# Gate and up by seven block products, tokens stationary in the output, gate/up and down products

## The chip, the cores and the metric

One core of one Trainium2 chip runs the whole program. The metric is the device time of one execution in microseconds (us); three runs of the kernel before gave 935.81, 935.91 and 936.03 us, median 935.91 us. The engines are TensorE (PE, with its weight loads as PEld), VectorE (DVE), ScalarE (ACT), GpSimd (POOL) and SyncE (SP, which here only issues transfers). SBUF is the on-chip memory, PSUM the eight banks into which TensorE writes; one bank holds a 128x512 float32 tile.

## The reference

512 tokens of width 1024, one layer, float32. What matters here are the last steps:

```
h   = x + merged @ w_out                      # w_out 1024x1024
xn  = rmsnorm(h) * norm_ffn
hid = silu(xn @ w_gate) * (xn @ w_up)         # both 1024x2816
y   = h + hid @ w_down                        # w_down 2816x1024
out = rmsnorm(y) * norm_final
```

Ahead of them stand an input projection 1024 wide to 7184 columns, three recurrent mixers and three branch projections merged with sigmoid gates. Those are the same in both kernels.

## The kernel before, in words

Every product of large matrices is computed in three passes. A float32 operand is split into a high part (a cast to a shorter float format, by ACT, line 73) and a low part (operand minus high part, by DVE, line 74); `mm3` (lines 100 to 103) adds high*high, high*low and low*high in PSUM. A weight chunk is 128x1024 (512 KB): `wdma` (line 83) loads it into one of three buffers `wraw`, `wsplit` (line 86) splits it into one of three buffers `whi` and `wlo`. So a transfer waits until an older chunk has been split, and a split waits until TensorE is done with an older chunk.

Up to the merge the features lie on partitions and the tokens, 512 of them, are what streams. From there to the end it stays so: for each of eight feature tiles `hsrc` (line 648) takes one weight chunk, does 24 matmuls of 128x512 with the weight block as the stationary side, adds the residual (line 656), multiplies by the norm weight, splits (lines 665 to 668) and adds up squares. Then for each of 22 hidden tiles, gate and up each take one chunk and 24 matmuls (lines 678 to 685), 1056 in all; the row norm's factor is formed beside the first of them (lines 686 to 691) and applied after the product (line 693). The hidden tile is split at once (line 699). The down product takes 66 matmuls for each of eight feature tiles (line 738); the last of these tiles is done in two halves of 256 tokens (`products`, line 744), so that the final norm of the first half and its output lie beside the second. The second half is transposed on TensorE (line 775), scaled and written out.

The program is written once as a stream; a planner then orders it for each engine. It gives an engine, at each point of its own planned time, the ready instruction that stands first in the written order. An instruction whose buffer is still held, or whose input is planned to come later, is passed over, and later written work goes ahead of it. The chip then runs each engine's list strictly in that order.

Of the kernel before, what the change touches and what calls it, by code (L numbers as in the profile page):

```python
# [21 lines left out]
TK = (5, 11)  # L22
# [17 lines left out]
OUT_SHAPE = (2, L * D // 2)  # L40

# columns of the small-vector table
# [5 lines left out]
def trunk_kernel(ctx: ExitStack, tc: tile.TileContext, xT, vecs, w_main, w_v, w_r, w_gk, w_br, w_out, w_gu,  # L48
                 w_down, masks, diag, rot, out):
    nc = tc.nc  # L50
    cpool = ctx.enter_context(tc.tile_pool(name="cpool", bufs=1))
    xpool = ctx.enter_context(tc.tile_pool(name="xpool", bufs=1))
    wpool = ctx.enter_context(tc.tile_pool(name="wpool", bufs=3))
    tpool = ctx.enter_context(tc.tile_pool(name="tpool", bufs=8))
    spool = ctx.enter_context(tc.tile_pool(name="spool", bufs=39))
    mix = ExitStack()
    mpool = mix.enter_context(tc.tile_pool(name="mpool", bufs=2))
    psp = ctx.enter_context(tc.tile_pool(name="psp", bufs=4, space=bass.MemoryType.PSUM))
# [74 lines left out]
    def col(i):  # L133
        return vec[:, i:i + 1]

# [31 lines left out]
    uh, ul = [], []  # L167
    S1 = tpool.tile([P, L], F32, tag="ssum", name="ssum", bufs=1)
# [130 lines left out]
    def carried(ks, qsel, lam, pa, vs, h0, pos):  # L299
        """ks: one tile per head, or one tile holding both heads; lam: a state's decay over each tile, or None"""  # L300
# [42 lines left out]
    # a pair of heads: two full-height heads (A), or two half-height heads in one tile with the queries  # L343
    # laid out block-diagonally (C)
# [6 lines left out]
    def gated(qs, ks, fs, vs, h0, pos):  # L351
# [12 lines left out]
        tots = [tpool.tile([P, L], F32, tag="tot", name="tot", bufs=2) for _ in fs]  # L364
# [9 lines left out]
        else:  # L374
            # an even token's own score comes with level 2, an odd one's with level 4, where keys are still as they were
# [72 lines left out]
    def head_out(pss, gn, gs, o, h0):  # L448
        """normalise over each head's values (tokens on partitions), turn, scale, gate, split"""
# [196 lines left out]
    hT = []  # L646

    def hsrc(dt):
        wh, wl = wload(w_out[dt], KT, P)
        xr = temp(name="xres")  # L650
        nc.scalar.dma_start(xr, xT[:, dt, :])
        ps = psj()
        for kt in range(KT):
            mm3(ps, wh[:, kt, :], wl[:, kt, :], mh[kt], ml[kt], kt == 0, kt == KT - 1)
        h = slot(name="hT")
        nc.vector.tensor_tensor(h, ps, xr, op=ALU.add)
        hT.append(h)
        return h

    xh, xl = [], []  # L660
    S2 = tpool.tile([P, L], F32, tag="ssum", name="ssum", bufs=1)
    for dt in range(KT):
        h = hsrc(dt)
        xw = temp(name="xw")
        nc.vector.tensor_scalar(xw, h, col(V_NFFN + dt), None, op0=ALU.mult)
        hi = xpool.tile([P, L], F32R, tag=f"xh{dt}", name=f"xh{dt}")
        lo = xpool.tile([P, L], F32R, tag=f"xl{dt}", name=f"xl{dt}")
        split(xw, hi, lo)
        xh.append(hi)
        xl.append(lo)  # L670
        add_square(S2, h, dt == 0)
    rc2 = cpool.tile([P, NT], F32, tag="rc2", name="rc2")
    R2 = xpool.tile([P, L], F32, tag="R", name="R2")

# [1 line left out]
    hpool = ctx.enter_context(tc.tile_pool(name="hpool", bufs=16))  # L676
    hid = []
    for ft in range(FT):
        pss = []
        for g in range(2):  # L680
            wh, wl = wload(w_gu[g, ft], KT, P)
            ps = psj()
            for kt in range(KT):
                mm3(ps, wh[:, kt, :], wl[:, kt, :], xh[kt], xl[kt], kt == 0, kt == KT - 1)
            pss.append(ps)
            if ft == 0 and g == 0:
                ss2 = psm((P, NT))
                sumsq(ss2, S2, True, True)
                rroot(ss2, D, rc2)
            elif ft == 0:  # L690
                nc.scalar.copy(R2, bcast(rc2))
        z = temp(name="fz")
        nc.vector.tensor_tensor(z, pss[0], R2, op=ALU.mult)  # L693
        nc.scalar.activation(z, z, AF.Silu)
        hr = temp(name="hr")
        nc.vector.tensor_tensor(hr, pss[1], z, op=ALU.mult)  # L696
        a = slot(dtype=F32R, name="hh")
        b = hpool.tile([P, L], F32R, tag="h", name="hl") if ft < 16 else slot(dtype=F32R, name="hl")
        split(hr, a, b)
        hid.append((a, b))  # L700

# [1 line left out]
    HW = L // 2  # L703
    out_f = out[0].rearrange("(k p l) -> k p l", p=P, l=HW)
    out_t = out[1].rearrange("(t p d) -> t p d", p=P, d=D)
    ss3 = [psm((P, 2)) for _ in range(2)]
    r3 = [cpool.tile([P, 2], F32, tag=f"r3{i}", name=f"r3{i}") for i in range(2)]
    parts = ((0, 8), (8, 15), (15, 22))

    S3 = tpool.tile([P, L], F32, tag="ssum", name="ssum", bufs=1)  # L710

    def residual(ps, dt, cs):
        d = temp((P, cs.stop - cs.start), name="d")
        nc.vector.tensor_tensor(d, ps, R2[:, cs], op=ALU.mult)
        nc.vector.tensor_tensor(hT[dt][:, cs], d, hT[dt][:, cs], op=ALU.add)
        if dt < KT - 1:
            add_square(S3, hT[dt], dt == 0)
            return None
        sq = temp((P, HW), name="sq")
        nc.vector.tensor_tensor(sq, hT[dt][:, cs], hT[dt][:, cs], op=ALU.mult)  # L720
        return sq

    def mean(half, sq):
        sumsq(ss3[half], S3[:, half * HW:half * HW + HW], True, False)
        sumsq(ss3[half], sq, False, True)
        rroot(ss3[half], D, r3[half])

    for dt in range(KT):
        ws = []
        last = dt == KT - 1  # L730
        if not last:
            ps = psj()
        for lo, hi in parts:
            wh, wl = wload(w_down[dt, :, lo:hi, :], hi - lo, P)
            ws.append((wh, wl))
            if not last:
                for kt in range(lo, hi):
                    mm3(ps, wh[:, kt - lo, :], wl[:, kt - lo, :], hid[kt][0], hid[kt][1], kt == 0, kt == FT - 1)
        if not last:
            residual(ps, dt, slice(0, L))  # L740
            continue
        pss = [psj((P, HW)) for _ in range(2)]

        def products(half, k0, k1):
            cs = slice(half * HW, half * HW + HW)
            for (lo, hi), (wh, wl) in zip(parts, ws):
                for kt in range(max(lo, k0), min(hi, k1)):
                    mm3(pss[half], wh[:, kt - lo, :], wl[:, kt - lo, :], hid[kt][0][:, cs], hid[kt][1][:, cs],
                        kt == 0, kt == FT - 1)

        products(0, 0, FT)
        sq = residual(pss[0], dt, slice(0, HW))
        products(1, 0, TK[0])
        mean(0, sq)
        products(1, TK[0], TK[1])
        rb = bcast(r3[0])
        for d in range(KT):
            y = temp((P, HW), name="y")
            nc.vector.scalar_tensor_tensor(y, hT[d][:, :HW], col(V_NFIN + d), rb, op0=ALU.mult, op1=ALU.mult)
            (nc.scalar if d % 2 else nc.sync).dma_start(out_f[d], y)  # L760
# [17 lines left out]
        for d in range(KT - 1):  # L778
            turn(d)
# [101 lines left out]
```

## Time and profile before

| what | us |
|---|---|
| median of three runs | 935.91 |
| span of the profiled execution, first to last instruction | 933.8 |
| output projection, from 517.3 | 43.6 |
| gate and up, from 560.9 | 241.2 |
| down product, from 802.1 | 121.9 |
| end, from 924.0 | 9.8 |
| TensorE busy over the span | 921.1 |
| DVE busy over the span | 442.2 |
| ACT busy over the span | 306.7 |

For the profiled execution only the span is listed; the median of the runs lies 2.1 us above it (start and finish that the records don't hold). In the profile, the busy time of a matmul is modelled and overlaps that of the next, so the pace of TensorE is read from the starts of neighbouring matmuls. "Idle before" and "waits" name what an engine waited for last.

### The profile page before, as it was taken

The numbers are of one execution on the slowest core, as the hardware profiler recorded it, in microseconds if no ns is written. First come the engines' busy times: TensorE is split into PE (matmuls) and PEld (weight loads), VectorE is DVE, ScalarE is ACT, GpSimd is POOL, SyncE is SP. The second block draws the span as 40 slices with busy tenths as digits, with TensorE's granted clock in tenths as the row PEclk, the third lists the DMA queues.
The fourth block names the chain that finished last, engine by engine and source line by source line (L and its number), as shares of the span: only waits on it lengthen the run. The fifth ranks groups of instructions, "written<-read, shape, count | busy, mean of one in ns | idle before, by whom it ended". The sixth has DMA issues, their size and how long they took to land.

```text
span 933.8 us, 11094 instructions
## 1 busy us (share of the span) xinstructions
PE 921.1 (99%) x4520; PEld 764.7 (82%) x4520; DVE 442.2 (47%) x637; ACT 306.7 (33%) x431; POOL 76.3 (8%) x68
## 2 busy tenths in 40 slices
PE   8999999999999999999999999999999999999996
PEld 7888878888878878888888888888888888888886
DVE  7924555666453664445343564444344344233333
ACT  6444338234323223222233433332232232222220
POOL 2101102123000000111122000000000000000000
PEclk9999999999999999999999999999999999999999
DMA  8332211232221222222232452222322322323312
GB/s 289 115 113 91 91 46 46 68 91 91 91 71 65 91 68 68 91 68 68 91 113 90 132 153 93 98 91 97 107 91 91 111 92 85 105 82 105 98 46 91
DMA packets 27843, 88.26 MB, mean 95 GB/s; under 512 B 3440, under 2 KB 4880, under 8 KB 27792
## 3 DMA queue, kind: packets, MB, share of 16 engines
q1 hardware_dynamic: 25264, 83.36, 27.6%
q10 hardware_dynamic: 2016, 3.15, 1.1%
q0 software_dynamic: 512, 1.05, 0.5%
q8 instruction: 35, 0.57, 0.2%
q14 instruction: 16, 0.13, 0.0%
HBM read 84.39 MB, written 2.10 MB: 93 GB/s over the span
## 4 chain that ended last, share of the span: by engine, by line
PE 94%; DVE 2%; issue 2%; DMA 1%; ACT 1%; SPq 0%; POOLq 0%; POOL 0%; DVEq 0%; ACTq 0%
PE pj L101 26%; PE pj L102 26%; PE pj L103 26%; PE pj L234 5%; PE pm L361 1%; PE pm L358 1%; PE pm L336 1%; PE pm L234 1%; PE pm L339 1%; DMA xraw<-in_xT_dram 1%; PE pm L397 1%; ACT whi L73 1%; PE pm L469 1%; DVE pta L411 0%; DVE wlo L74 0%
## 5 line engine op out<-in xcount | busy, mean ns | idle before, releaser
L73 ACT CAST whi<-wraw 128x1024 fp32r<-128x1024 f32 (+1 forms) x153 | 158.3, 1035 | 505.2 <-PE pj L102 350.0
L101 PE MATMUL pj<-xh,whi 128*128 128x512 f32 x768 | 302.4, 394 | 0.0
L102 PE MATMUL pj<-xl,whi 128*128 128x512 f32 x768 | 299.9, 391 | 0.0
L103 PE MATMUL pj<-xh,wlo 128*128 128x512 f32 x768 | 299.5, 390 | 0.0
L74 DVE TENSOR_TENSOR wlo<-wraw,whi 128x1024 fp32r<-128x1024 f32 (+1 forms) x153 | 188.3, 1232 | 211.1 <-ACT whi L73 206.5
L103 PEld LDWEIGHTS pj<-xh,wlo 128*128 128x128 f32 x768 | 144.2, 188 | 30.0
L101 PEld LDWEIGHTS pj<-xh,whi 128*128 128x128 f32 x768 | 144.3, 188 | 29.7 <-issue 0.3
L102 PEld LDWEIGHTS pj<-xl,whi 128*128 128x128 f32 x768 | 144.3, 188 | 28.8
L101 PE MATMUL pj<-hh,whi 128*128 128x512 f32 (+1 forms) x198 | 72.5, 366 | 0.0
L103 PE MATMUL pj<-hh,wlo 128*128 128x512 f32 (+1 forms) x198 | 72.4, 365 | 0.0
L102 PE MATMUL pj<-hl,whi 128*128 128x512 f32 (+1 forms) x198 | 72.4, 365 | 0.0
L696 DVE TENSOR_TENSOR hr<-pj,fz 128x512 f32<-128x512 f32 x22 | 15.2, 692 | 72.0 <-PE pj L103 71.3
L103 PEld LDWEIGHTS pj<-hh,wlo 128*128 128x128 f32 x198 | 37.3, 189 | 6.0
L102 PEld LDWEIGHTS pj<-hl,whi 128*128 128x128 f32 x198 | 37.4, 189 | 6.0
L101 PEld LDWEIGHTS pj<-hh,whi 128*128 128x128 f32 x198 | 37.3, 189 | 6.0
L693 DVE TENSOR_TENSOR fz<-pj,R 128x512 f32<-128x512 f32 x22 | 15.2, 691 | 55.0 <-PE pj L103 55.0
L101 PE MATMUL pj<-oh,whi 128*128 128x512 f32 x96 | 38.7, 403 | 0.0
L102 PE MATMUL pj<-ol,whi 128*128 128x512 f32 x96 | 37.5, 391 | 0.0
L103 PE MATMUL pj<-oh,wlo 128*128 128x512 f32 x96 | 37.5, 391 | 0.0
L509 POOL TENSOR_TENSOR mrg<-mrg,mt 128x512 f32<-128x512 f32 x16 | 24.7, 1545 | 121.1 <-DVE mt L508 121.1
L147 POOL TENSOR_TENSOR r<-rm,mhalf 128x2 f32<-128x2 f32 x2 | 1.4, 696 | 357.5 <-DVE rm L146 357.5
L101 PE MATMUL pj<-mh,whi 128*128 128x512 f32 x64 | 24.9, 389 | 0.0
(207 smaller groups left out, 968.7 us busy)
## 6 DMA issues: line engine op xcount, KB each, us to landing
wraw<-in_w_main_dram SPq DMA_DIRECT2D x52, 512.0 KB, 3.3
wraw<-in_w_gu_dram SPq DMA_DIRECT2D x44, 512.0 KB, 3.3
wraw<-in_w_down_dram SPq DMA_DIRECT2D x16, 448.0 KB, 3.3
wraw<-in_w_br_dram SPq DMA_DIRECT2D x12, 512.0 KB, 3.3
wraw<-in_w_v_dram SPq DMA_DIRECT2D x11, 512.0 KB, 4.3
wraw<-in_w_out_dram SPq DMA_DIRECT2D x8, 512.0 KB, 3.5
wraw<-in_w_down_dram SPq DMA_DIRECT2D x8, 512.0 KB, 3.5
xraw<-in_xT_dram SPq DMA_DIRECT2D x8, 256.0 KB, 6.0
```

The lines of the kernel that those rows point to most:

```text
L73: a = nc.scalar.copy(hi, raw)
L74: b = nc.vector.tensor_tensor(lo, raw, hi.bitcast(F32), op=ALU.subtract)
L101: nc.tensor.matmul(ps, lhsT=ah, rhs=bh, start=start, stop=False)
L102: nc.tensor.matmul(ps, lhsT=ah, rhs=bl, start=False, stop=False)
L103: nc.tensor.matmul(ps, lhsT=al, rhs=bh, start=False, stop=stop)
L234: nc.tensor.matmul(pss[t], lhsT=a[kt][:, t * P:(t + 1) * P], rhs=b[:, k, :], start=kt == 0 and n == 0, stop=kt == KT - 1 and n == 2)
L336: nc.tensor.matmul(ps[:, t, :], lhsT=pa[:, h, t, :], rhs=vs[t][:, hs], start=t == 0, stop=False)
L339: nc.tensor.matmul(ps[:, t, :], lhsT=q, rhs=sts[h % n][r, t - 1, :], start=False, stop=t == NT - 1)
L358: nc.tensor.matmul(out, lhsT=ks[0][:, j], rhs=isel(qs[0]), start=True, stop=True)
L509: nc.gpsimd.tensor_tensor(mrg[dt], mrg[dt], t, op=ALU.add)
L693: nc.vector.tensor_tensor(z, pss[0], R2, op=ALU.mult)
L696: nc.vector.tensor_tensor(hr, pss[1], z, op=ALU.mult)
```

## The change

After the merge the sides of the products are swapped: a block of 128 tokens is the stationary side, and 512 (or 256) columns of the weights stream. Three stages are rewritten.

Output projection: two halves of 256 tokens, each with four PSUM banks (two token tiles by two column halves) filled over eight chunks of `w_out`. All of `w_out` is so loaded and split twice. `hnat` adds the residual, spills h to memory (8 transfers of 256 KB on the POOL queue), `hturn` transposes it back (32 transposes in all) with the norm weight applied by ACT.

Gate and up: the normalised input is cut into a 2x2 grid (token halves by halves of the 1024 inputs), the weights into a 2x2 grid (halves of the inputs by gate and up). Seven block products replace the eight, on sums of blocks. Four sums of token blocks are formed once (`combine`), and with the three plain blocks that are used they are split (`form`); four sums of weight blocks are formed on DVE for each 512 hidden columns. Hidden columns are taken in five jobs of 512 and one of 256. Each product is 24 matmuls; partial results pass between PSUM banks by ACT copies (`seed`) and DVE additions (`after`). The hidden tiles come out with tokens on partitions, and `turn_hid` transposes them (88 transposes in all).

Down product: per token half, 22 chunks of `w_down`, 12 matmuls each, all of `w_down` loaded and split twice; the hidden tiles are split here, by halves. In the second half the last four chunks are kept, so that one token tile ends before the other. Squares come from ACT with a running sum, `finish` scales and writes.

The pool of the earlier stages (`spool`, 39 tiles) is closed after the token blocks are split; the weights' second buffers `wr2`, the weight sums `wv` and the hidden tiles take its memory and wait for its tiles one by one.

```diff
+    def combine(a, b, flip=False):
+        out = []
+        for g in range(2):
+            s = slot(name="xs")
+            if flip:
+                nc.vector.scalar_tensor_tensor(s, a[g], -1.0, b[g], op0=ALU.mult, op1=ALU.subtract)
+            else:
+                nc.vector.tensor_tensor(s, a[g], b[g], op=ALU.subtract)
+            out.append(s)
+        return out
...
+    PRODUCTS = {"P1": ("11", "11"), "P2": ("12", "21"), "P5": ("R1", "V1"), "P6": ("F2", "V2"), "P7": ("S3", "V3"),
+                "P3": ("F4", "22"), "P4": ("22", "V4")}
+    SUMS = {"V1": ("11", "12"), "V2": ("V1", "22"), "V3": ("12", "22"), "V4": ("V2", "21")}
...
+        for p in ("P1", "P2", "P5", "P6", "P7", "P3", "P4") if j == 0 else ("P1", "P5", "P6", "P2", "P7", "P3", "P4"):
+            steps.append((j, p))
...
+    def prep(j, p):
...
+            if name in SUMS:
+                a, b = (live[j, s + g] for s in SUMS[name])
+                v = fw.tile([P, 1024], F32, tag="wv", name="wv", bufs=4)
+                nc.vector.tensor_tensor(v, a, b, op=ALU.add)
...
+            split(r, hi, lo)
...
+    for kt, _ in enumerate(oproj(1, second_half)):
+        if kt == 1:
+            hsquares(0, hs)
+        if 1 <= kt < 5:
+            c, g = turns[kt - 1]
+            hturn(0, hs, c, g, psj())
+            if g:
+                form("1" + "12"[c], block(0, c))
+        if kt == 5:
+            prep(0, "P1")
+    hs = hnat(1, second_half)
...
+    product(0, "P1", A, True)
+    after(0, "P1")
+    for c, g in turns:
+        hturn(1, hs, c, g, psm())
+    r1 = combine(block(1, 1), block(1, 0))
+    form("R1", r1)
+    s3 = combine(block(0, 0), block(1, 0))
+    f2 = combine(s3, block(1, 1), True)
+    form("F2", f2)
+    form("S3", s3)
+    form("F4", combine(f2, block(0, 1), True))
+    form("22", block(1, 1))
+    hsquares(1, hs)
+    late.close()
...
+    prep(*steps[1])
+    for i in range(1, len(steps)):
+        j, p = steps[i]
+        if i + 1 < len(steps):
+            prep(*steps[i + 1])
+        product(j, p, bank_of(p), p in ("P1", "P5"))
+        after(j, p)
+        if p in ("P1", "P5"):
+            turn_hid()
+            turn_hid()
```

In `product`, each product takes its weights in two halves a and b of 12 matmuls (one half for the last job). `after` does two 128x512 ACT copies behind P1, P5 and P7, two DVE additions behind P6 and P7, two Silu (ACT) behind P2 and P4, and two gated multiplications (DVE) each behind P3 and P4.

## Rows read from the trace of the kernel before

**Rows 1.** Windows: length, busy PE, PEld, DVE, ACT, POOL, clock, DMA share, GB/s.

```profile
15.00:20.00 5.00, 5.00 (x24) 4.12 (x23) 5.00 (x10) 4.75 (x11) 1.49 (x1) 1.00 1.03 399
...
517.30:560.90 43.60, 43.60 (x194) 36.03 (x193) 26.61 (x37) 16.43 (x24) 2.33 (x1) 1.00 0.52 156
560.90:802.10 241.20, 241.20 (x1074) 200.03 (x1073) 98.94 (x114) 72.44 (x92) 1.02 (x1) 1.00 0.29 96
802.10:924.00 121.90, 121.90 (x608) 103.92 (x607) 44.42 (x57) 29.38 (x37) 0.70 (x1) 1.00 0.28 82
```

**Rows 2.** The chain of waits: share by engine, then pieces (start, length).

```profile
PE 94%; DVE 2%; issue 2%; DMA 1%; ACT 1%; SPq 0%; POOLq 0%; POOL 0%; DVEq 0%; ACTq 0%
...
34.60 2.72 PE pj L234 x12
...
440.42 0.87 PE pm L469 x8
...
566.44 0.79 PE pm L140 x8
...
572.83 0.89 PE pm L155 x8
```

**Rows 3.** Timeline of TensorE: start, length, line; neighbouring 128x512 and 128x256 matmuls.

```profile
498.73 0.39 PE L103 MATMUL pj<-oh,wlo 128*128 128x512 f32 x1
498.96 0.39 PE L101 MATMUL pj<-oh,whi 128*128 128x512 f32 x1
...
912.05 0.28 PE L103 MATMUL pj<-hh,wlo 128*128 128x256 f32 x1
912.17 0.28 PE L101 MATMUL pj<-hh,whi 128*128 128x256 f32 x1
```

**Rows 4.** Groups by shape, gate and up window: busy us, mean ns, idle before.

```profile
L74 DVE TENSOR_TENSOR wlo<-wraw,whi 128x1024 fp32r<-128x1024 f32 x43 | 52.7, 1225 | 10.7 <-ACT whi L73 7.9
L73 ACT CAST whi<-wraw 128x1024 fp32r<-128x1024 f32 x43 | 45.3, 1054 | 163.5 <-PE pj L102 83.0 <-issue 80.5
L696 DVE TENSOR_TENSOR hr<-pj,fz 128x512 f32<-128x512 f32 x21 | 14.5, 692 | 68.4 <-PE pj L103 67.6 <-ACT fz L694 0.7
L74 DVE TENSOR_TENSOR hl<-hr,hh 128x512 fp32r<-128x512 f32 x21 | 14.4, 685 | 0.7 <-ACT hh L73 0.7
L691 ACT COPY R<-pm 128x512 f32<-128x512 f32 x1 | 0.6, 592 | 0.0
```

**Rows 5.** Groups by shape, whole span.

```profile
L764 ACT ACTIVATE hw<-hT,vec 128x256 f32<-128x256 f32 x7 | 3.4, 492 | 0.0
```

**Rows 6.** Timeline of DVE and ACT in the output projection.

```profile
534.96 1.22 DVE L74 TENSOR_TENSOR wlo<-wraw,whi 128x1024 fp32r<-128x1024 f32 x1
...
535.14 0.61 ACT L73 CAST xh<-xw 128x512 fp32r<-128x512 f32 x1
...
536.10 0.69 DVE L74 TENSOR_TENSOR xl<-xw,xh 128x512 fp32r<-128x512 f32 x1
```

**Rows 7.** Transfers: tile, queue, count, size, median us to landing.

```profile
wraw<-in_w_gu_dram SPq DMA_DIRECT2D x44, 512.0 KB, 3.3
...
out_dram<-y ACTq DMA_DIRECT2D x2, 256.0 KB, 3.3
```

**Rows 8.** Windows at the end, columns as in rows 1.

```profile
926.00:927.00 1.00, 0.69 (x6) 0.45 (x5) 0.16 (x1) 0.00 (x0) 0.31 (x1) 1.00 0.00 0
...
930.00:931.00 1.00, 0.00 (x0) 0.00 (x0) 0.00 (x0) 0.00 (x0) 0.00 (x0) 1.00 1.02 383
931.00:932.00 1.00, 0.00 (x0) 0.00 (x0) 0.00 (x0) 0.00 (x0) 0.00 (x0) 0.53 0.79 287
```

**Rows 9.** Timeline of the end: last matmul, mean, root, scaling, transfers.

```profile
923.82 0.28 PE L103 MATMUL pj<-hh,wlo 128*128 128x256 f32 x1
...
926.69 0.70 POOL L147 TENSOR_TENSOR r<-rm,mhalf 128x2 f32<-128x2 f32 x1 [8.28 <-DVE rm L146]
...
928.20 1.00 ACTq L789 DMA_DIRECT2D out_dram<-y  x2
```

More of the change, by code (lines that the diff above doesn't have):

```diff
@@ L363, in gated @@
         cur = [f[:, :] for f in fs]
[L364 removed]
+        tots = [mpool.tile([P, L], F32, tag="tot", name="tot", bufs=2) for _ in fs]
         if wide:
@@ L662, in trunk_kernel @@
[L662 to L673, printed above, removed]
@@ L676, in trunk_kernel @@
[L676 to L700, printed above, removed]
@@ L703, in trunk_kernel @@
[L703 to L721, printed above, removed]
@@ new lines, in hnat @@
+    def hnat(H, pss):
+        hs = []
+        for c in range(2):
+            row = []
+            for tl in range(2):
+                t = 2 * H + tl
+                xr = temp(name="xres")
+                nc.sync.dma_start(xr, x[t, :, c * HALF:(c + 1) * HALF])
+                h = slot(name="hn")
+                nc.vector.tensor_tensor(h, pss[tl][c], xr, op=ALU.add)
+                nc.gpsimd.dma_start(hspill[t, c], h)
+                row.append(h)
+            hs.append(row)
+        return hs
@@ new lines, in form @@
+    def form(name, parts):
+        hi = xform.tile([P, 4, 256], F32R, tag=f"h{name}", name="fh")
+        lo = xform.tile([P, 4, 256], F32R, tag=f"l{name}", name="fl")
+        for g in range(2):
+            split(parts[g].rearrange("p (k t) -> p k t", t=256), hi[:, 2 * g:2 * g + 2], lo[:, 2 * g:2 * g + 2])
+        forms[name] = (hi, lo)
+    def combine(a, b, flip=False):
+        out = []
+        for g in range(2):
+            s = slot(name="xs")
[5 more added lines that the diff above has]
+        return out
@@ new lines, in trunk_kernel, with product @@
+    A = B = E = None
+    def product(j, p, banks, start):
+        n = JOBS[j]
+        f, name = PRODUCTS[p]
+        fh, fl = forms[f]
+        gs = groups(j)
+        k = 4 // len(gs)
+        for gi, g in enumerate(gs):
+            wh, wl = (t.rearrange("p (k n) -> p k n", n=n) for t in live[j, "p" + name + g])
+            for tl in range(2):
+                ts = slice(tl * P, (tl + 1) * P)
+                for kk in range(k):
+                    kt = gi * k + kk
+                    for q, (x_, w_) in enumerate(((fh, wh), (fl, wh), (fh, wl))):
+                        nc.tensor.matmul(banks[tl][:, :n], lhsT=x_[:, kt, ts], rhs=w_[:, kk, :],
+                                         start=start and kt == 0 and q == 0, stop=kt == 3 and q == 2,
+                                         skip_group_check=True)
@@ new lines, in trunk_kernel, with turn_hid, silu @@
+    hidT, pending = [], []
+    def turn_hid():
+        if not pending:
+            return
+        hn, i = pending.pop(0)
+        ps = psm()
+        for t in range(NT):
+            nc.tensor.transpose(ps[:, t * P:(t + 1) * P], hn[t][:, i * P:(i + 1) * P], dg[:, 0, :])
+        r = fw.tile([P, L], F32, tag="hid", name="hid", bufs=FT)
+        nc.scalar.copy(r, ps)
+        hidT.append(r)
+    def silu(bank, n, t):
+        z = temp(name="fz")
+        nc.scalar.activation(z[:, :n], bank[:, :n], AF.Silu, scale=rc2[:, t:t + 1])
+        return z
@@ new lines, in trunk_kernel @@
+    hs = hnat(1, second_half)
+    A, B = [psj() for _ in range(2)], [psj() for _ in range(2)]
+    for tl in range(2):
+        nc.tensor.matmul(B[tl], lhsT=forms["11"][0][:, 0, :P], rhs=live[0, "p11a"][0][:, :512], start=True, stop=True)
+    product(0, "P1", A, True)
[6 more added lines that the diff above has]
+    f2 = combine(s3, block(1, 1), True)
@@ new lines, in trunk_kernel @@
+    form("F2", f2)
[4 more added lines that the diff above has]
+    late.close()
+    fw = late2.enter_context(tc.tile_pool(name="fw", bufs=1, side="right", reuse_waits="tile"))
+    m2 = cpool.tile([P, NT], F32, tag="m2", name="m2")
+    nc.vector.tensor_tensor(m2, ss2[:, :NT], ss2[:, NT:], op=ALU.add)
+    rroot(m2, D, rc2)
+    nc.gpsimd.tensor_scalar(nrc2, rc2, -1.0, 0.0, op0=ALU.mult, op1=ALU.add)
+    E = [psm() for _ in range(2)]
```

276 lines of the change are left out of this document (191 added, 85 removed).

## The prediction

> **What bounds the kernel now.** First the windows by stage: in the three stages that are rewritten TensorE is busy for the whole of 43.6, 241.2 and 121.9 us, while DVE has work for 26.6, 98.9 and 44.4 us and ACT for less [rows 1]. Then the chain of waits: 94% of it is TensorE, and no other engine holds more than 2% [rows 2]. So in these stages time is the number of matmuls by their pace. Their modelled length (0.39 us) is not the pace; the starts of neighbours are. They stand 0.23 us apart at 512 columns, and twelve with weights streaming take 2.72 us, which is 0.2267 us each; at 256 columns the step is 0.12 us [rows 2, 3]. In the twelve of 2.72 us the tokens already are the stationary side, so turning the sides round costs nothing by itself. Then the groups of DVE and ACT, because all that the change adds beside the matmuls falls on these two [rows 4, 5].
>
> **TensorE, step by step.**
> Gate and up: 1056 matmuls at 0.2267 are 239.4 us. After: five jobs of 7 x 24 at 0.2267 (190.4 us), one of 7 x 24 at 0.12 (20.2 us), 210.6 us in all: -28.8 us. The last job falls short of half by 1.1 us, because 0.12 is more than half of 0.2267.
> Transposes: 32 of h and 88 of hidden tiles. Eight took 0.87 us on the chain [rows 2], 0.11 each: +13.2 us. All stand in TensorE's order between matmuls, so none is hidden.
> Two matmuls that only open the banks B: +0.45 us.
> Gone: the row norm's sums and its spread beside the first gate product, 0.79 and 0.89 us [rows 2]: -1.7 us.
> Down product: 121.9 us now [rows 1], of which the last feature tile pays 132 steps of 0.12 and two norm steps. After, 528 at 0.2267 are 119.7 us: -2.2 us.
> The output projection keeps its 192 matmuls: 0.
> The end: from the last matmul at 923.82 to the start of the last transfers at 928.20 are 4.4 us, two per queue [rows 9]. After: addition 0.69, squares 0.6, two small DVE steps of some 0.2, root 0.70, two scalings of 0.7 and some six hand-overs of 0.1 are 4.4 us too, but the last transfer (3.3 us [rows 7]) has none ahead of it in its queue: -0.4 us (-1 to +1).
> Sum of TensorE's work: -28.8 + 13.2 + 0.45 - 1.7 - 2.2 - 0.4 = -19.45 us.
>
> **The output projection's supply.** A chunk now serves 12 matmuls, 2.72 us, where it served 24. Per chunk ACT needs 1.05 and DVE 1.23 [rows 4]; landing, cast and subtraction make 3.3 + 1.05 + 1.23 = 5.6 us for three buffers [rows 4, 7], 1.9 us a chunk. 512 KB in 2.72 us is 193 GB/s, where one window of before moved 399 GB/s [rows 1]. That holds in the down product too, where the hidden tile's split adds about half of 0.69 to DVE. Near the end of the second half the first product's two weight halves hold two of three buffers, and the last two chunks stand out: cast and subtraction behind the freed buffer, 2.3 us, then a late transfer on top, 3.2 us. The first product's 24 matmuls (5.44 us) are ready and can go in between: the trace shows the planner doing such a thing, a later chunk's subtraction at 534.96 ahead of the token tile's at 536.10, whose cast came only at 535.14 [rows 6]. I take 0 (0 to 5.4).
>
> **The crossing into gate and up, the one large stall.** When the output projection ends, DVE owes: 8 combinations and 10 low parts of 128x512, 18 x 0.69 = 12.4 us; one low part for P2 (1.23; its other half's buffer may lie free early); for P5 two additions and a low part of 128x1024, 3.7 us, an SBUF addition being priced as the subtraction of that size [rows 4]. That is 17.3 us. It can begin about 1.6 us in: the last residual additions, then the 16 transposes (1.8 us) and ACT's scalings at 0.49 each [rows 5], of which the first two must land. Add 0.7 for gaps, since the four scaled tiles come 0.9 us apart: P5 starts at about 19.6 us. TensorE has 1.76 us of transposes and P2, 5.44 us, for that time. Stall: 12.4 us. It does not matter for the sum whether P2 goes early or late. Before, there was no stall here. From below, 7 us: DVE fits low parts into the gaps and P5's needs ahead of S3, F4 and 22; what is then late next are those forms, as DVE carries job 0's own 30 us besides. From above, 17: a second-buffer load waits for a tile of the closed pool, then 3.3 us to land.
>
> [...]
>
> **Gate and up in steady state.** Per job of 512, TensorE: 168 x 0.2267 + 16 x 0.11 = 39.8 us. DVE: 14 low parts and 8 additions at 1.225, 8 steps on PSUM at 0.69: 32.5 us. ACT: 14 casts at 1.054 and 14 copies or Silus at about 0.59: 23.1 us [rows 4]. So DVE goes from 41% of the stage [rows 1] to 82% and stays below TensorE. Its worst window is the one behind P6 or P7: two PSUM steps, two additions and two low parts make 6.3 us against a product of 5.44. But the additions may be done a product earlier: four buffers, and the products between need 2.5 us. Three split buffers for two halves a product leave each half one product's length, 5.4 us, for 1.05 + 1.23 and its turn on DVE. In the window from 15 to 20 us DVE was busy all 5.00 us and TensorE too [rows 1], so a full DVE doesn't by itself stop it. Loss: at best 0; the upper bound is 12, a third of a microsecond for each of 38.5 products. I take 2. Transfers: 4 MB a job, 105 GB/s, no limit.
>
> Crossing into the down product: the banks B are free once the last Silu (0.6 us) has read them: +0.5 (0 to 2). The spill, 8 transfers, and its reading back lie beside products.
>
> **Sum.** -19.45 + 12.4 + 2 + 2 + 0.5 = -2.55 us on the profiled span of 933.8: 931.25. The runs' median lies 2.1 us above that span, and I carry that over: 933.4 us.
>
> **Rivals.**
> A, the crossing is covered. For it: DVE has room while the second half of the output projection runs, and ACT is half idle there [rows 1]. Against it: the tiles that it needs exist only after that half. With 7 for 12.4 and no clock loss: 933.4 - 5.4 - 2 = 926.0. Chance 0.20.
> B, slower: DVE becomes the bound in gate and up. It runs in strict order and waits for ACT's cast ahead of each low part (7.9 us over 43 now [rows 4]) and for TensorE ahead of each PSUM step. Its slack is 39.8 - 32.5 = 7.3 us a job, 1.04 us a product; beyond that it sets the pace. If standing takes 1.3, each of 38.5 products loses 0.3: 11.5 us in place of 2, 943 us. It decides the sign from some 0.17 us a product on (another 4.4 us over 38.5 products, beside my 2). Against it: the window with DVE full. Chance 0.27.
> C, the loads hold the crossing: the second buffers' memory comes free only with the last forms, transfers stand in order on SP, and P2, P5 and P6 each wait. The upper end of 17 and the 2.3 and 3.2 us of the output projection unfilled: 933.4 + 4.6 + 5.4 = 943.4. Chance 0.08.
> My forecast, with the crossing at 10 to 15 us and gate and up keeping pace: 0.45, its own range 929 to 938.
>
> **How the numbers follow.** A run is told from no change beyond 0.2%, 1.9 us: below 934.0 or above 937.8. The forecast puts 0.25 below, 0.13 between, 0.07 above; A all 0.20 below; B and C about 0.05 between and below together, 0.30 above. Faster 0.46, same 0.17, slower 0.37. All low ends together make 923 (7 for 12.4, no clock, no loss, 1 at the end), all high ends 960. The range, 921 to 947, allows two more below for what no row shows, and leaves out the far end of B and C above.
>
> **What would show it.** TensorE: between the output projection and gate and up an idle stretch of about 12 us with DVE busy all through, and a clock of one half behind it; before the last two chunks of the output projection no gap. Per job some 40 us with DVE at 80% and TensorE without gaps; if TensorE's starts step by more than 0.2267 ahead of each product and its releaser is DVE's low part, it is B. From the start of the down product to the last matmul some 120 us. Wrong would be a crossing under 5 us, jobs above 42 us, or transposes away from 0.11.

## The result, and the profile after

The changed kernel takes 949.38 us (median of four runs, 948.47 to 949.98) against 935.92 of the kernel before on the same chip (four runs, 935.81 to 936.03): a ratio of 1.0143 (1.0128 to 1.0157). It is slower, by 13.5 us; the forecast was 933.4, and the range ended at 947. The profiled execution has a span of 946.7 us, 12.9 more than before.

First the windows of the changed kernel, cut where its stages begin; columns as in [rows 1].

```profile
0.00:526.26 526.26, 520.86 (x2626) 423.12 (x2627) 268.29 (x423) 186.87 (x278) 72.75 (x64) 1.00 0.27 89
526.26:580.97 54.71, 54.71 (x251) 44.02 (x249) 28.65 (x30) 29.37 (x49) 6.74 (x9) 1.00 0.64 219
580.97:601.60 20.63, 9.15 (x25) 6.85 (x25) 17.06 (x26) 11.59 (x22) 2.13 (x2) 0.67 0.42 150
601.60:816.80 215.20, 214.05 (x1048) 177.93 (x1046) 167.64 (x164) 120.63 (x156) 0.00 (x0) 1.00 0.29 98
816.80:939.70 122.90, 122.90 (x530) 99.45 (x530) 77.44 (x106) 62.20 (x100) 1.86 (x3) 1.00 0.62 202
610.00:810.00 200.00, 199.88 (x965) 165.83 (x964) 154.81 (x151) 109.78 (x141) 0.00 (x0) 1.00 0.29 98
...
590.00:595.00 5.00, 0.47 (x1) 0.47 (x2) 5.00 (x10) 2.17 (x3) 0.36 (x1) 0.50 0.12 31
595.00:600.00 5.00, 5.00 (x14) 3.90 (x14) 3.88 (x4) 1.05 (x1) 1.77 (x2) 0.53 0.99 351
```

The first line is the surprise. Up to the output projection nothing was rewritten, and that part takes 526.3 us where it took 517.3 [rows 1]: +9.0. From there to the down product it is 290.5 against 284.8 (+5.7), the down product 122.9 against 121.9 (+1.0), and the end 7.0 against 9.8 (-2.8). Together +12.9. So two thirds of the loss stand where the diff has no computation, at a granted clock of 1.00 and with TensorE as busy as before (520.86 of 526.26 us, 511.72 of 517.30 before).

The chain of waits (start, length) shows what is slower there:

```profile
PE 93%; DVE 3%; ACT 1%; issue 1%; DMA 1%; SPq 0%; DVEq 0%; POOLq 0%; ACTq 0%
...
32.31 2.81 PE pm L238 x12
35.12 2.82 PE pj L238 x12
37.94 2.81 PE pm L238 x12
```

Twelve products take 2.81 us that took 2.72 [rows 2]. It is the same at every stage: over the whole trace the mean step from the start of one 512-column matmul to the next (steps over 300 ns left out) is 232.7 ns, before it was 227.2. On some 3,340 products 5.6 ns make up to 18.7 us, more than the whole loss. What the two kernels differ in there is where the operands lie. Before, in all but 18 of these products (small ones of the mixers) the program's addresses put both operands 64 bytes above a multiple of 256: normed tokens from 21056, weights from 55872, slots (the tiles of `spool`) from 115520. In the changed kernel the small constant tiles take 64 bytes more, the pools stand in another order and the slots are packed from the top of memory: weights begin at 128 above a multiple of 256, tokens at 0, slots at 224.

The crossing into gate and up, the timeline of TensorE:

```profile
579.06 1.91 PE L694 MATMUL pm<-dg,hn 128*128 128x128 f32 x16
587.69 0.80 PE L793 MATMUL pj<-whi,fh 128*128 128x512 f32 x1 [6.72 <-ACT whi L77]
...
589.13 0.63 PE L793 MATMUL pj<-whi,fl 128*128 128x512 f32 x1
594.53 0.80 PE L793 MATMUL pj<-wlo,fh 128*128 128x512 f32 x1 [4.76 <-DVE wlo L78]
595.12 0.63 PE L793 MATMUL pj<-whi,fh 128*128 128x512 f32 x1
595.54 0.63 PE L793 MATMUL pj<-whi,fl 128*128 128x512 f32 x1
...
599.76 0.39 PE L793 MATMUL pj<-wlo,fh 128*128 128x512 f32 x1
```

Two waits, 6.72 and 4.76 us, stand ahead of P2's products, and the products behind them step by 0.43 us until 599.4. The window 580.97 to 601.60 above holds only P2: 20.6 us for 5.4 us of work. The last two windows show why: DVE is busy for all 5.00 us in which TensorE has one product, and the granted clock is at 0.50 and 0.53.

Gate and up by groups, for the window 601.6 to 816.8 (busy us, mean ns, idle before):

```profile
L78 DVE TENSOR_TENSOR wlo<-wv,whi 128x1024 fp32r<-128x1024 f32 x43 | 52.5, 1223 | 22.2 <-ACT whi L77 21.1 <-PE pm L806 0.5
L77 ACT CAST whi<-wv 128x1024 fp32r<-128x1024 f32 x43 | 45.0, 1050 | 40.8 <-PE pj L793 28.4 <-PE pm L793 10.4 <-issue 1.3
L806 PE MATMUL pm<-dg,hnat 128*128 128x128 f32 x88 | 11.7, 272 | 0.0
```

The split of a weight sum costs what the split of a loaded weight cost (1223 ns on DVE and 1050 on ACT, 1225 and 1054 [rows 4]), and ACT still waits for TensorE, not the other way round.

### The profile page after: what moved, and what is told of

It reads as the page before. It is cut to its first block, busy times and chain, and to the rows that moved or that the text cites. A ratio compares the mean times of both kernels' runs of the same rounds, so it can differ in the third digit from the quotient of the medians.

```text
span 946.7 us, 11541 instructions
## 1 busy us (share of the span) xinstructions
PE 921.7 (97%) x4476; PEld 751.4 (79%) x4476; DVE 561.5 (59%) x752; ACT 411.4 (43%) x602; POOL 84.0 (9%) x79
## 4 chain that ended last, share of the span: by engine, by line
PE 93%; DVE 3%; ACT 1%; issue 1%; DMA 1%; SPq 0%; DVEq 0%; POOLq 0%; ACTq 0%
PE pj L793 16%; PE pj L105 15%; PE pj L106 15%; PE pj L107 15%; PE pm L793 6%; PE pj L238 5%; PE pm L105 3%; PE pm L107 3%; PE pm L106 3%; PE pm L365 1%; PE pm L362 1%; PE pm L238 1%; PE pm L340 1%; PE pm L343 1%; PE pm L806 1%
## 5 line engine op out<-in xcount | busy, mean ns | idle before, releaser
L105 PE MATMUL pj<-xh,whi 128*128 128x512 f32 x416 | 167.2, 402 | 0.0
L106 PE MATMUL pj<-xl,whi 128*128 128x512 f32 x416 | 164.8, 396 | 0.0
L107 PE MATMUL pj<-xh,wlo 128*128 128x512 f32 x416 | 164.7, 396 | 0.0
L793 PE MATMUL pj<-whi,fh 128*128 128x512 f32 (+1 forms) x240 | 92.4, 385 | 6.8 <-ACT whi L77 6.7
L793 PE MATMUL pj<-wlo,fh 128*128 128x512 f32 (+1 forms) x240 | 90.9, 380 | 4.8 <-DVE wlo L78 4.8
L107 PEld LDWEIGHTS pj<-xh,wlo 128*128 128x128 f32 x416 | 78.3, 188 | 18.0
L105 PEld LDWEIGHTS pj<-xh,whi 128*128 128x128 f32 x416 | 78.3, 188 | 17.6 <-issue 0.3
L106 PEld LDWEIGHTS pj<-xl,whi 128*128 128x128 f32 x416 | 78.4, 188 | 17.3
L793 PE MATMUL pj<-whi,fl 128*128 128x512 f32 (+1 forms) x240 | 91.5, 381 | 0.0
L78 DVE TENSOR_TENSOR wlo<-wv,whi 128x1024 fp32r<-128x1024 f32 x44 | 53.7, 1223 | 22.2 <-ACT whi L77 21.1
L77 ACT CAST whi<-wv 128x1024 fp32r<-128x1024 f32 x44 | 46.1, 1050 | 46.4 <-PE pj L793 28.4
```

What stands on the lines that cost most here:

```text
L77: a = nc.scalar.copy(hi, raw)
L78: b = nc.vector.tensor_tensor(lo, raw, hi.bitcast(F32), op=ALU.subtract)
L105: nc.tensor.matmul(ps, lhsT=ah, rhs=bh, start=start, stop=False)
L106: nc.tensor.matmul(ps, lhsT=ah, rhs=bl, start=False, stop=False)
L107: nc.tensor.matmul(ps, lhsT=al, rhs=bh, start=False, stop=stop)
L793: nc.tensor.matmul(banks[tl][:, :n], lhsT=x_[:, kt, ts], rhs=w_[:, kk, :], start=start and kt == 0 and q == 0, stop=kt == 3 and q == 2, sk ...
```

## The experiments

Theory T says that the pace of a 512-column product depends on whether its two operands begin at the same offset within 256 bytes. Its rivals: the offset of one operand alone counts (R1), or the slower pace has nothing to do with offsets (R2: other engines, the region of memory).

**e1, matmuls alone.** A kernel of its own: 64 groups of 24 products, every pairing of eight offsets. In short:

```
for a in RES: for b in RES:      # 0, 32, ... 224 bytes: moving, stationary
    24 x matmul(ps, lhsT=sta[:, b/4 + 128*(n%7):], rhs=mov[:, a/4 + 512*(n%3):])
```

> A kernel of matmuls alone (it computes nothing of the reference): 64 groups of 24 products of a 128x128 stationary and a 128x512 moving tile, fp32r, with all other engines idle. The moving operand begins 0, 32, ... 224 bytes behind a fixed place, the stationary one likewise, every pairing once. Theory T (the pace of a 512-column product depends on whether both operands begin at the same offset within 256 bytes; in the kernel before both do, at 64; in the changed kernel they begin 128, 96 or 32 apart): about 227 ns from start to start in the pairs with equal offsets, 232 to 234 ns in the others. Rival R1 (the offset of one operand alone counts, whatever the other's): fast rows or fast columns in the 8 by 8 table instead of a diagonal. Rival R2 (the slower pace comes from what the other engines and the DMAs do at the same time, or from the region the tiles lie in): one pace in all 64 groups.

Mean step in ns, worked out from the starts in its trace (inside each group, steps at the lower clock left out), rows the moving operand's offset, columns the stationary one's:

```
        0     32     64     96    128    160    192    224
  0  228.4  233.2  233.3  234.1  233.4  233.5  229.0  233.2
 32  233.3  227.7  233.2  233.3  234.1  233.3  233.5  229.0
 64  228.8  233.3  226.6  233.2  233.3  234.1  233.3  233.5
 96  233.3  228.9  233.3  226.7  233.2  233.4  234.1  233.3
128  233.3  233.5  229.0  233.3  226.7  233.2  233.4  234.1
160  234.0  232.4  233.2  228.9  233.2  226.6  233.2  233.3
192  233.4  234.1  233.3  233.5  229.0  233.3  226.7  233.2
224  232.8  233.3  234.1  233.3  233.5  229.0  233.3  226.7
```

The diagonal is fast (226.6 to 228.4 ns), and the table repeats along it (232.4 to 234.1 at all other differences but one), so in these 64 pairs only the difference of the offsets counts, modulo 256. R1 would have shown fast rows or columns, R2 one number; DVE, ACT and POOL had no work in this stretch:

```profile
40.00:300.00 260.00, 260.00 (x1122) 210.34 (x1121) 0.00 (x0) 0.00 (x0) 0.00 (x0) 1.00 0.00 1
```

One other difference is nearly as fast: a stationary operand that begins 192 bytes above the moving one (modulo 256), 228.8 to 229.0. That was not expected.

**e2, the changed kernel with its operands aligned.**

```
+    edge = ctx.enter_context(tc.tile_pool(name="edge", bufs=1, side="right"))
+    edge.tile([P, 56], F32, tag="pad", name="pad")
+    cpool.tile([P, 32], F32, tag="pad", name="pad")
+    tpool.tile([P, 32], F32, tag="pad", name="pad", bufs=1)
     late = ExitStack()
```

> The changed kernel with three unused tiles added (128 bytes behind the constants, 128 bytes behind the temporaries, 224 bytes at the top of memory), so that all operands of the 512-column products begin at offset 0 within 256 bytes; no instruction differs. Theory T: the step goes from 232.3 to 227 ns in all stages, 3,340 products x 5.4 ns = 18 us, so 930 to 932 us, and the first output projection at 517 us again instead of 526. Rival R2 (traffic of other engines, region of memory): 949 us, step 232, the first output projection at 526.

Measured: 932.71 us (931.91 to 933.46), 0.9968 of before (0.9955 to 0.9981), that is 16.7 us less than the changed kernel for three unused tiles, and a little above the 930 to 932 that were expected. The step is back at 227 ns in its chain (twelve products of the front, 24 of gate and up, eight transposes); below that its windows:

```profile
35.49 2.72 PE pj L242 x12
...
649.18 5.44 PE pm L797 x24
...
665.51 0.87 PE pm L810 x8
```

```profile
0.00:518.14 518.14, 511.90 (x2627) 421.95 (x2627) 269.20 (x423) 186.51 (x278) 71.65 (x64) 1.00 0.26 91
518.14:571.70 53.56, 53.56 (x251) 43.87 (x249) 28.63 (x30) 29.12 (x48) 6.72 (x9) 1.00 0.65 223
571.70:592.00 20.30, 8.79 (x26) 6.54 (x26) 17.17 (x26) 11.68 (x22) 3.21 (x2) 0.66 0.39 149
592.00:803.26 211.26, 209.98 (x1047) 177.58 (x1045) 166.47 (x164) 120.79 (x156) 0.00 (x0) 1.00 0.29 101
803.26:923.80 120.54, 120.53 (x530) 99.07 (x530) 77.51 (x106) 62.37 (x100) 1.86 (x3) 1.00 0.58 205
610.00:800.00 190.00, 190.00 (x954) 161.51 (x954) 147.06 (x146) 107.08 (x138) 0.00 (x0) 1.00 0.28 95
```

Against the changed kernel's windows the front gives back 8.1 us, the stretch up to the down product 5.4 and the down product 2.4. The crossing is as long as it was. No instruction differs, only the pace, and the 16 us between the two spans (946.7 and 930.8) are its price.

**e3, the kernel before with its weights shifted.**

```
+    gap = ctx.enter_context(tc.tile_pool(name="gap", bufs=1))
+    gap.tile([P, 32], F32, tag="pad", name="pad")
     wpool = ctx.enter_context(tc.tile_pool(name="wpool", bufs=3))
```

> The kernel before with one unused tile of 128 bytes ahead of the weight buffers: the weights and all that lies behind them begin at offset 192 within 256 bytes, the normed activations (xh, xl) stay at 64. 2,400 products then pair 192 with 64 (the first projections, gate and up), 1,134 pair 192 with 192 (output and down projections and some of the first). Theory T (equal offsets are fast, whatever they are): the 2,400 step at 232 to 233, the others stay at 227; 2,400 x 5.5 = +13 us, so 949 us; the loss stands before the output projection and in gate and up, none in the output projection (517.3:560.9 before) and the down projection. Rival R1 (offset 64 itself is fast): all 3,534 slower, +19 us, 955 us. Rival R2: 936 us, no change.

Measured: 949.93 us, 1.0155 of before (1.0138 to 1.0172). The rewriting isn't needed to get the loss. Windows by stage:

```profile
0.00:524.48 524.48, 518.57 (x2627) 422.18 (x2627) 269.28 (x423) 186.30 (x278) 71.60 (x64) 1.00 0.26 90
524.48:568.20 43.72, 43.72 (x194) 36.16 (x193) 26.61 (x37) 16.53 (x24) 2.33 (x1) 1.00 0.52 154
568.20:815.90 247.70, 247.70 (x1071) 199.62 (x1070) 98.95 (x114) 72.37 (x91) 1.02 (x1) 1.00 0.27 93
815.90:937.90 122.00, 122.00 (x607) 103.91 (x606) 44.42 (x57) 29.40 (x37) 0.69 (x1) 1.00 0.27 81
```

The two stages whose pairs stayed equal (192 with 192) keep their 43.7 and 122.0 us [rows 1]; the front (+7.2) and gate and up (+6.5), where 2,400 products became pairs of 64 with 192, pay. That is the contrast inside one kernel that T asked for, and it refutes R1, by which all four would pay.

**e4 and e11, which pair it is.** Both are matmuls alone. e4 tries offsets of 4 bytes and pairs that alternate; `group` takes the offsets of the moving and of the stationary tile. In short:

```
for b in range(0, 64, 4): group((0,), (b,))
group((0, 128), (0, 128)); group((0, 128), (128, 0)); group((0,), (0, 128))
group((0,), (0,), 256); group((0,), (128,), 256)
```

> A kernel of matmuls alone (it computes nothing of the reference), 24 products a group, fp32r. First 16 groups: moving tile at offset 0, stationary tile 0, 4, 8, ... 60 bytes behind it. Then pairs of offsets that alternate from product to product: (0 with 0, 128 with 128), where each product has equal offsets but its stationary tile differs from the moving tile of the product before; (0 with 128, 128 with 0), where it is the other way round; and moving always 0 with stationary 0, 128, 0, .... Then 256 columns at equal offsets and 128 apart. Theory T as run e1 left it: only equal offsets are fast, so 227 ns in the first group and 233 from 4 bytes on; rival: the offset counts in steps of 32 bytes, so 227 up to 28 and 233 from 32 on. For the alternating groups, theory T1 (a tile of weights is read while the product before it still streams, so a stationary tile has to match the moving tile of the product ahead of it): 233 in the first alternating group, 227 in the second. Rival T2 (a product's own two operands have to match): 227 in the first, 233 in the second. With 256 columns the time lost is the same 5.5 ns (113 to 119 ns) if it is lost at the change of weights, half of it if it is lost along the columns.

Four bytes are enough: 232.3 ns at 4, and 230 to 235 at all others up to 60, where the group with equal offsets that was measured last settles at 227. The alternating groups came out at 236.7 (own pair equal) and 230.0 (own pair unequal): the order that T1 asks for, but 3 to 4 ns above it in both. At 256 columns the one unequal pair that was tried is not slower, 120.0 equal and 118.4 unequal: both terms of the expectation are wrong. e11 lets the pair change only every twelve products:

```
run((0, 0), (0, 0)); run((0, 0), (128, 128)); run((0, 0), (0, 128)); run((0, 0), (128, 0))
```

> A kernel of matmuls alone (it computes nothing of the reference): four stretches of 384 products, 128x512 fp32r, in which twelve products with one pair of offsets (moving, stationary) follow twelve with another: (0,0) throughout; (0,0) and (128,128); (0,0) and (0,128); (0,0) and (128,0). Read is the mean step from each of the 24 places to the next. Theory T1 (what counts is the stationary tile of the next product against the moving tile that streams): in the second stretch the steps at places 11 and 23, where the pair changes, are slow (over 230 ns) and the other 22 at 227; in the third the slow ones are 11 to 22, not 12 to 23. Rival T2 (a product's own pair counts): no slow step in the second stretch, and 12 to 23 in the third. In the fourth both have 12 to 23 slow.

```
(0,0)/(128,128), median step in ns at the places 0 to 23:
231 227 226 227 227 226 227 227 226 227 227 232   231 227 226 227 227 226 227 227 226 227 227 232
```

T2 is out, since each product's own pair is equal here. The step ahead of a change is slow (232), as T1 says, but the step behind it is slow too (231). In the third stretch places 11 to 22 are slow as T1 has it (228 to 241), but 23 is too (233), and places 0 to 6 (224 to 236) stand before the pace settles at 227 from 7 on. In the fourth, places 12 to 23, slow by both theories, swing between 224 and 238, and places 0 to 2 (231 to 233) are slow too. So T1 is nearer, but not the whole rule. Why the slow steps last so long stays open.

**e5, the forms left out.** On e2's kernel. The crossing was forecast as DVE's work for the forms.

```
-    r1 = combine(block(1, 1), block(1, 0))
...
-    form("22", block(1, 1))
+    for name in ("R1", "F2", "S3", "F4", "22"):
+        forms[name] = forms["12"]
```

> The aligned changed kernel (932.7 us) without the five forms of the second half of the tokens: R1, F2, S3, F4 and 22 are not computed, and their products read the form 12 instead, so the result is not the reference's. It leaves 8 combinations and 10 splits (8 x 0.64 + 10 x 0.61 = 11.2 us of DVE, 10 casts of 0.57 of ACT) out of the crossing from the output projection into gate and up. Theory D (P2's and V1's weights wait in line behind the forms on ACT and DVE, the prediction's own): the two waits of TensorE there, 6.75 and 4.76 us, and most of the 2.9 us that its lower clock costs behind them are gone; 14 us in all, 919 to 922 us. Rival L (the weights' loads come late, whatever DVE does): they land some 4 us behind their issue at 566.4 to 567 us, at most 1 us behind the end of the transposes, so they would have to hold 10 us more for buffers; then 929 to 933 us.

Measured: 926.57 us, 6.1 less than e2, between the two expectations. TensorE's waits fell from 6.75 and 4.76 to 3.56 and 2.14. The timeline of ACT tells what is left:

```profile
570.28 3.00 ACT L701 ACTIVATE xa<-pm,vec 128x256 f32<-128x256 f32 x8
573.13 0.67 ACT L691 ACTIVATE sq<-hn 128x512 f32<-128x512 f32 x1
573.65 0.24 ACT L691 ACTIVATION_READ_ACCUMULATOR sq<-hn 128x1 f32 x1
573.75 1.08 ACT L81 CAST whi<-wraw 128x1024 fp32r<-128x1024 f32 x1
...
581.74 1.28 ACT L817 ACT_TABLE_LOAD   x1 [5.97 <-PE pj L797]
583.04 0.69 ACT L817 ACTIVATE fz<-pj,rc 128x512 f32<-128x512 f32 x1
583.62 1.98 ACT L81 CAST whi<-wv 128x1024 fp32r<-128x1024 f32 x2
```

P2's cast stands behind the scalings and squares, V1's behind a SiLU that waits for P2 itself. So DVE's forms are not the whole of the stall: ACT's line is a second cause below them.

**e6, TensorE or DVE in gate and up (rival B).** On e2's kernel:

```
-        product(j, p, bank_of(p), p in ("P1", "P5"))
+        if p != "P7":
+            product(j, p, bank_of(p), p in ("P1", "P5"))
```

> The aligned changed kernel without the 24 matmuls of P7 in each of the six jobs; its weight sum, cast and split still run, so the load of DVE and ACT stays (the result is not the reference's). Theory P (gate and up are bound by TensorE; the forecast): 5 x 24 x 0.2268 + 24 x 0.12 = 30.1 us less, 902 to 903.5 us, since DVE with 147 of 190 us busy in 610:800 would have 147 of 163. Rival B (DVE holds the pace in gate and up): DVE and ACT have the same work as before, so less than 15 us comes off, 918 us or more.

Measured: 905.08 us, 27.6 less than e2. A window of its gate and up:

```profile
610.00:770.00 160.00, 159.62 (x793) 134.23 (x792) 142.31 (x142) 103.25 (x135) 0.00 (x0) 1.00 0.32 110
```

With the same work on DVE in fewer microseconds (89% busy instead of 77%) TensorE still waits for 0.4 us of 160 only. B is refuted for the jobs after the first; a product is worth nearly what its matmuls take (30.1 us expected). Most of the 2.5 us that are missing are four waits for DVE of 0.3 to 0.9 us in the first job, 2.0 us in all, between 596 and 613 us, where e2 has one of 0.2: there, just behind the crossing, DVE does run late.

**e7, e8, e10, weights ahead of the forms; e9, both.** e7 loads P2's weights and V1's second term into room that is free at the crossing:

```
+    early = early_x.enter_context(tc.tile_pool(name="early", bufs=1, reuse_waits="tile"))
...
     after(0, "P1")
+    prep(*steps[1])
     for c, g in turns:
         hturn(1, hs, c, g, psm())
+    product(0, "P2", B, False)
+    prep(*steps[2])
```

> The aligned changed kernel with another order at the crossing: P2's weights (21) and V1's second term (12) are loaded into four buffers of their own in the room that is free there (132352 to 148736), P2's split and V1's sum (in place, into the raw tile of 11) are written ahead of the forms of the second half, and 12 and 21 are loaded a second time for V3 and V4. Nothing is left out. Theory D: P2 follows the transposes with no wait, so that the two waits (6.75 and 4.76 us) and 2.9 us of lower clock go; DVE then has, from 565 us on, 12.4 us of work ahead of P5 and about 8.7, 6.1, 5 and 6.1 us ahead of each product after it against 5.4 us of TensorE each, so 2 to 5 us of new waits come in the first job: 932.7 - 14.4 + 3.5 = 922 us, 919 to 926. Rival L: the loads set it, then the new buffers alone do the same. Rival S (the planner puts the forms ahead of V1 again, or DVE is late for P5 and P6 by as much as it was for P2): 928 to 933 us.

Measured: 927.44 us, 0.9910 of before (0.9893 to 0.9926): 5.3 less than e2, above D's range (919 to 926) and just below S's. P2 and P5 had no wait to speak of, and then the timelines of TensorE and of SP's queue and the list of SP's waits show the next:

```profile
590.66 0.80 PE L801 MATMUL pj<-whi,fh 128*128 128x512 f32 x1 [8.07 <-ACT whi L81]
```

```profile
566.07 20.92 SPq L764 DMA_DIRECT2D wr<-in_w_gu_dram  x5
```

```profile
SPq L764 <- DVE fl L82: 18.6, 1, 18.6
```

Five loads in SP's line took 20.9 us to go out, 18.6 of them behind the low part of a form: by the program's addresses two of the first four tiles so loaded lie on scaled token tiles that the forms still read. That is the mechanism of the prediction's rival C, the loads. It was there in e2 already, as the timeline of SP's queue and the list of DVE's waits show:

```profile
566.75 19.20 SPq L760 DMA_DIRECT2D wr<-in_w_gu_dram  x5
```

```profile
DVE wv L773 <- DMA wr<-in_w_gu_dram: 1.8, 3, 1.0
```

DVE itself reached the sums of these tiles so late that it waited only 1.8 us for them; the loads became the limit once DVE's line was out of the way. e9 takes both causes away at once, e7's order and e5's omission:

> Run e7's kernel and run e5's omission together: P2's and V1's weights early, and the five forms of the second half not computed (the result is not the reference's). Theory D3 (e5 saved 6 us and not 14 because P2's cast still stood behind 6 us of ACT's work on the transposes and squares, and V1's behind the first SiLU; e7 saved 5 us because the forms then held the tiles that the loads of 22 need; either is met by the other): no wait of over 1 us is left at the crossing, and the whole 14.9 us goes: 918 us, 917 to 920. Rival (the two savings are the same 5 to 6 us, and what is left is something third): 925 to 927 us.

918.16 us, as expected, 14.6 less than e2. Its largest waits of TensorE from 560 to 625 us:

```profile
581.75 0.50 PE L801 MATMUL pj<-whi,fh 128*128 128x512 f32 x1 [0.32 <-ACT whi L81]
588.25 0.47 PE L801 MATMUL pj<-whi,fh 128*128 128x512 f32 x1 [0.41 <-DVE pm L847]
```

So the stall is worth 14.6 us, and neither the forms (6.1) nor the order (5.3) frees it alone. e8 carries the order on to P6; `steps[3]` is P6, whose V2 is summed in place, with 22 from the early buffers:

```
+    product(0, "P5", E, True)
+    after(0, "P5")
+    prep(*steps[3])
...
     s3 = combine(block(0, 0), block(1, 0))
```

> Run e7's kernel (927.4 us, where TensorE waited 8.07 us ahead of P6, for the cast of V2, and stepped at the lower clock for some 5 us behind that) with 22 loaded into the early buffers too, V2 summed in place in V1's tile, and P5 and V2's split written ahead of the forms S3, F4 and 22; 12, 21 and 22 are loaded a second time. Theory D2 (P6 waited for the load of 22, which was issued only when the forms had given their tiles free at 584 to 587 us, and for DVE behind it): DVE then reaches V2's second split at about 585 us instead of 592, so P6 starts about 2 us late instead of 8, and the clock stays up: 927.4 - 6 - 2.5 = 919 us, 917 to 922. Rival W (the wait only moves on by one product again, to P7, whose sum takes 12 and 22 from tiles that come free at the same time as before): 925 to 928 us.

928.33 us: no gain over e7, and just above W's 925 to 928. W was right. P6 had no wait over 0.4 us, and P7 had the same one, on the same kind of load (timeline of DVE, then of TensorE):

```profile
595.65 2.42 DVE L777 TENSOR_TENSOR wv<-wr,wr 128x1024 f32<-128x1024 f32 x2 [4.35 <-DMA wr<-in_w_gu_dram]
```

```profile
598.07 0.79 PE L801 MATMUL pj<-whi,fh 128*128 128x512 f32 x1 [8.26 <-ACT whi L81]
```

e10 does it to the end, V3 (`steps[4]`) in place in 12's tile and P3's split of 22 (`steps[5]`) too, with P6 and P7 written between the forms:

```
     form("F2", f2)
+    product(0, "P6", A, False)
+    after(0, "P6")
+    prep(*steps[4])
     form("S3", s3)
...
+    product(0, "P7", A, False)
+    after(0, "P7")
+    prep(*steps[5])
+    form("F4", combine(f2, block(0, 1), True))
```

> Run e8's kernel carried through to the last product that the early buffers can feed: V3 is summed in place in the early tile of 12, P3's split of 22 reads its early tile, and the first job's products P6 and P7, the squares and the reciprocal root are written in the order P5, V2, F2, P6, V3, S3, squares, P7, 22's split, F4, form 22; 12, 21 and 22 are loaded a second time only for V4 and the second job's own loads. Nothing is left out. Theory D4 (each wait so far, 6.75 + 4.76 us ahead of P2, 8.07 us ahead of P6, 8.26 us ahead of P7, was a raw tile whose load waited for the forms' tiles to come free, with DVE's line behind it; with the loads gone from the line only DVE's sum is left: some 42 us of DVE work from 566 to 604 us against 33 us of TensorE's): no single wait of TensorE over 3 us between 565 and 610, 2 to 4 us of them in all, the clock at 1.00 throughout: 919 to 923 us. Rival W2 (the wait moves on once more, to P4, whose sum needs 21 from a tile that comes free at about 590 us): one wait of 6 to 8 us there and 926 to 929 us.

923.01 us (921.53 to 923.46), 0.9856 of before (0.9839 to 0.9872): the whole computation, at the top of D4's 919 to 923, and faster than both kernels. All of TensorE's waits between 545 and 620 us:

```profile
578.51 0.50 PE L801 MATMUL pm<-whi,fl 128*128 128x512 f32 x1 [1.17 <-DVE fl L82]
585.75 0.74 PE L801 MATMUL pj<-whi,fh 128*128 128x512 f32 x2 [1.97 <-ACT fh L81]
586.79 0.50 PE L801 MATMUL pj<-whi,fl 128*128 128x512 f32 x1 [0.30 <-DVE fl L82]
```

```profile
585.00:590.00 5.00, 3.94 (x11) 2.89 (x12) 5.00 (x9) 4.20 (x12) 0.00 (x0) 0.76 0.00 0
590.00:595.00 5.00, 5.00 (x21) 3.99 (x21) 3.34 (x6) 3.01 (x4) 0.42 (x1) 0.89 0.23 74
```

They make 3.4 us, as D4 had it; only the clock did not stay at 1.00 (0.76 and 0.89 for ten microseconds).

## Why the prediction was wrong

**The step that failed** is the pace. The prediction read 0.2267 us from [rows 2, 3] and used it for every product after, with the words "turning the sides round costs nothing by itself", and it priced the unchanged front at nothing. Turning the sides costs nothing indeed: in e2's gate and up, where the tokens are stationary, 24 products take 5.44 us. But the pace is no constant of the 512-column product. It held where both operands began at the same offset modulo 256 bytes (226.6 to 228.4 ns in e1, at the other differences 232.4 to 234.1, at one of them some 229), which was so in all but 18 of these products in the kernel before, and the diff moved the pools. That term was absent from the sum; e2 against the changed kernel gives it 16.7 us, e1 and e3 show that the offsets alone make it. With it the prediction's 933.4 becomes 950.1; measured were 949.4. No rival named it: B and C reach 943 by other causes.

**TensorE's work** was right as a sum, in part by luck. In e2, where the pace is the old one, the span is 3.0 us under before's, forecast were 2.55. Of its parts, eight transposes take 0.87 us, 0.11 each as forecast. The down product gained 1.4 instead of 2.2, with two of the hidden tiles' turns inside it. The end gained 2.8 instead of 0.4: from the end of the last product to the end of the span 7.0 us, where it was 9.8 [rows 1, 9]. There the steps up to the last issue took the 4.4 us of the forecast (923.41 to 927.83 in e2), but only two transfers of 256 KB stand behind them and the span ends 3.0 us later; with four of them it ended 5.6 us after 928.20 [rows 9]. The front lost 0.8, all of it by the 51st matmul at 15 us, while the first inputs are still landing; its cause is open. So 2.4 us more at the end cover what the other parts fell short.

**The crossing** was right in size: 12.4 and 2 forecast; measured in e2 20.3 us for P2's 5.4, so 14.9, of which 11.5 are waits (6.75 and 4.76) and the rest the products at the lower granted clock (0.50 from 580 to 585 us, 0.55 from 585 to 590). Its cause was only partly right. The prediction counted DVE's line and put the stall ahead of P5; it stood ahead of and inside P2. The runs show three things in a row: ACT's line, DVE's forms, and loads that wait for the forms' tiles (the prediction's upper end and its rival C). Without forms 6.1 us come back, with early weights 5.3, with both 14.6. "It does not matter for the sum whether P2 goes early or late" held in part: with P2 early (e7) 5.3 us came back, and the wait that was left moved to P6 and in e8 to P7.

**The clock.** The first 2 us of the sum stand for a lower clock behind the stall; they were the author's estimate, and no run shows them. In their place the changed kernel's trace shows a clock of one half behind the stall, as expected. TensorE's transposes ended at 580.97; the granted clock was 1.00 from 585 to 586 us, 0.51 from 586 to 587, 0.50 from 594 to 599, 0.66 from 599 to 600 and 1.00 from 600 to 605. Products ran from 587.69, waited at 589.8, began again at 594.53 and stepped at 0.23 us from 599.8 on. The 16 products between stepped at some 0.43 us, 0.2 us more than behind them, so the lower clock cost about 3 us, an estimate from these steps.

**Gate and up in steady state** lost 0.1 us of 200 (window 610 to 810), and 1.2 us in the whole window from 601.60, forecast 2; DVE stands at 77%, forecast 82%. Rival B did not occur: e6 shows TensorE almost without waits even with DVE at 89%. The supply of the output projection was right at 0: P1's products filled the gaps of its last two chunks, and the window 526.26 to 580.97 has no idle time.

## What to carry to other kernels

Where time is products times pace, the pace belongs to the placement as well as to the instruction (226.6 to 234.1 ns for the same product in e1): when a change adds or moves buffers, compare the start offsets of the two operands (modulo 256 bytes) before and after, and compare a stage that the change does not touch first. Three unused tiles were worth 16.7 us of 949 here. And where a stage begins with preparation on other engines, look for every line that the preparation stands in: here a single cause removed moved the wait on by one product (8.07 us ahead of P6 in e7, 8.26 ahead of P7 in e8), and only all of them together gave 9.7 of 14.6 us back.

## What the runs showed of the hardware

- In e1 a 512-column fp32r product stepped by 226.6 to 228.4 ns when its moving and stationary operands began at the same offset modulo 256 bytes, by 232.4 to 234.1 at the other multiples of 32 bytes, and by 228.8 to 229.0 when the stationary one began 192 above. Four bytes of difference were enough, 232.3 ns (e4).
- At 256 columns the one unequal pair that was tried (128 bytes apart) showed no such loss: 120.0 ns equal, 118.4 unequal (e4).
- It is not a matter of a product's own pair alone: with equal pairs throughout, the steps on both sides of a change of offset took 231 to 232 ns, and after twelve unequal pairs the pace needed three to seven products to settle (e11). What mechanism holds it that long no run here shows.
